# Gating normalizations put in order, two output tiles computed by token halves, and rotary tables started after the second latent weight

## The chip, the cores and the metric

The kernel runs on one core of a Trainium2 chip. The metric is the device time of one execution in microseconds (us). The engines of a core work side by side, each through its own queue in order: TensorE (PE, matmuls and transposes), VectorE (DVE), ScalarE (ACT), GpSimd (POOL) and SyncE (SP, which here only starts transfers). One engine waits for another by semaphores.

## The reference

Two layers run over a residual stream x of 1024 tokens by 1024 features, in float32.

```
for i in range(2):
    hn  = rms_norm(h, norm_mix[i])
    h  += mla(hn) if i == 0 else gmlp(hn)
    hn  = rms_norm(h, norm_ffn[i])
    h  += square(relu(hn @ ffn_w_up[i])) @ ffn_w_down[i]
    hn  = rms_norm(h, norm_ple[i])
    h  += sigmoid(hn @ ple_w_gate[i]) * (p[i] @ ple_w_proj[i])
```

Two parts matter here. The first is the start of `mla` (latent attention): `lat = hn @ w_down` gives 704 columns, 384 for the queries, 256 for keys and values, 64 for a rotary key; each part is normalized by its root mean square and the 64 are rotated by cos and sin of the token's position. The second is `gmlp`:

```
u, v = split(gelu(hn @ w_in))            # 2048 columns each
v  = layer_norm(v, ln_g, ln_b)           # over the 2048 columns of a token
sv = tril(w_s[g]) applied over the 128 tokens of a chunk, 8 groups g of 256 columns, + b_s
out = (u * sv) @ w_out
```

## The kernel before, in words

Every matrix is split into a high part of reduced float32 (fp32r) and a low part, the rest. A product is then three matmuls: high by high, high by low, low by high. `split(hi, lo, src)` does the splitting: ACT casts `src` to `hi` (line 111), DVE subtracts to get `lo` (line 112). A name that ends in h or l is such a part.

The program is written in one order and a scheduler of the language orders each engine's instructions from it, by priorities and estimated times; `tc.issue_after(ins)` is the one means by which the program itself pins what is issued under it behind a given instruction.

**Latent stage (first 50 us).** Eight blocks of 128 tokens: `block_x(b)` transposes a block on PE (tile `xp`, line 1088; two tiles of four transposes) and splits it (`xh`, `xl`); `square_x(b)` squares it on ACT (`xs`, line 1108) for the norm, and lets POOL add the parts (line 1109). `block_lat(b)` multiplies a block with the eight slices k of w_down (`lat`, line 65). Slice k of the weight is made when block 0 first needs it: ACT scales it to `wdh` (line 1065), DVE makes `wdl` (line 1066); of the last slice the two are one tile, `wdk`. Then ACT squares `lat` into `lats` with sums per token (line 1136), DVE turns the sums into reciprocal roots (`rl0v`, line 1496, with ACT's logarithm and exponential at 1497 and 1498) and scales `lats` (1141 to 1143), and `block_c(b)` transposes it on PE (`cp`, `cq`). The rotary tables come from `rope_tables`: DVE computes angles (`rw`, lines 1468 to 1472), ACT takes Abs and two Sin (1475 to 1477), DVE multiplies (`tab`, 1486 to 1489). A table load of ACT's function tables stands ahead of the Sins and another behind them (line 1288).

**Gating stage (about 1455 to 1915 us).** The second half of gelu(hn @ w_in), v, is computed first and parked in DRAM (`vpark`), with sums for the layer norm (`mv`, `rs`). Then four groups `gp` of 512 columns each run. Per group and block b of 128 tokens: `unit(b)` multiplies for u (`up`, ACT's gelu at line 894); `prep(b)` brings v back (`vr`, two blocks a transfer), normalizes it on DVE (line 884), multiplies by ln_g and adds ln_b on POOL (885, 886) and splits it into `vhl`; `spatial(b)` multiplies by w_s (`sv`) and DVE forms u·sv (line 908); `turn_y(b)` transposes that (`yp`, line 914) and splits it into `yh`, `yl`. At the end of a group `down_slice` multiplies yh, yl with four slices of w_out in eight output tiles `go` of 128 features by 1024 tokens, and DVE adds each into the residual (line 665). `go10` is group 1, tile 0. A matmul writes 512 tokens, so a tile has two halves c; a half needs the blocks 0 to 3 or 4 to 7 of y. `seq` makes the first tile of a group compute half 0 through all four k, and then half 1; every other tile does both halves at each k.

Of the kernel before, what the change touches and what calls it, by code (L numbers as in the profile page):

```python
# [16 lines left out]
P = 128  # L17
# [23 lines left out]
def trunk(ctx: ExitStack, tc: tile.TileContext, I, out):  # L41
# [68 lines left out]
    def split(hi, lo, src):  # L110
        S.copy(hi, src)  # L111
        V.tensor_tensor(lo, src, f32(hi), op=ALU.subtract)  # L112

# [24 lines left out]
    def gemm(blocks, rhs, f, name, seq=False, only=None):  # L138


        if only is not None:
            acc = {only: pso(name)}
            units = [(acc[only], CS[only])]
            csets = [(only,)]
        else:
            par[0] ^= 1
            if par[0]:
                full = psg(name)
                acc = [full[:, CS[c]] for c in range(2)]
                units = [(full, slice(0, T))] if not seq else [(acc[c], CS[c]) for c in range(2)]  # L150
            else:
                acc = [pso(f"{name}_{c}") for c in range(2)]
                units = [(acc[c], CS[c]) for c in range(2)]
            csets = [(0,), (1,)] if seq else [(0, 1)]
        nk = len(rhs)
        w = [(hi[:, kk, f * P:(f + 1) * P], lo[:, kk, f * P:(f + 1) * P]) for hi, lo in blocks for kk in range(hi.shape[1])]
        for cset in csets:
            for k, (wh, wl) in enumerate(w):
                for c in cset:
                    mm(acc[c], wh, rhs[k][c][0], k == 0, False)  # L160
                for c in cset:
                    mm(acc[c], wh, rhs[k][c][1], False, False)
                for c in cset:
                    mm(acc[c], wl, rhs[k][c][0], False, k == nk - 1)
        return units

    def chunked(hi, lo, n):
# [488 lines left out]
    def down_slice(w, k0, rhs, h, name, nxt, seq=False, before=None, after=None):  # L656
        bl = None
        for q in range(4):
            bl, ahead = bl or [load_block(w, k0, q * 256)], None
            for f in range(2):  # L660
                j = 2 * q + f
                if before is not None:
                    before(j)
                for u, c in gemm(bl, rhs, f, f"{name}{j}", seq and j == 0):
                    V.tensor_tensor(h[j][:, c], u, h[j][:, c], op=ALU.add)  # L665
# [116 lines left out]
    def gmlp(h, nrm, nxt, after):  # L782
# [83 lines left out]
        rs = rsqrt_small(mv[:, :, 1], EPS, "lnr")  # L866

        for gp in range(4):
            f0 = gp * 512
# [6 lines left out]
            vhl = tmp(f"vhl{gp}", [P, 2, 512], F32R)  # L876
            us, vr = {}, {}

            def prep(b):
# [3 lines left out]
                v = vr[0][:, b % 2]  # L883
                V.tensor_scalar(v, v, mv[:, b, 0:1], rs[:, b:b + 1], op0=ALU.subtract, op1=ALU.mult)
                G.tensor_tensor(v, v, gb[:, 0], op=ALU.mult)
                G.tensor_tensor(v, v, gb[:, 1], op=ALU.add)
                split(vhl[:, 0], vhl[:, 1], v)

# [21 lines left out]
            def turn_y(b):  # L910
# [4 lines left out]
                bs = slice(b * P, (b + 1) * P)  # L915
                split(yh[:, :, bs], yl[:, :, bs], pp.rearrange("p (j t) -> p j t", t=P))

# [84 lines left out]
    def mla(h, park):  # L1002
        w_down, w_uq, w_ukv, w_out = (I[n][0] for n in ("mla_w_down", "mla_w_uq", "mla_w_ukv", "mla_w_out"))
        with tc.tile_pool(name="pm", bufs=1) as pm:
# [108 lines left out]
            def block_lat(b):  # L1113
# [3 lines left out]
                for k in range(KT):  # L1117
# [10 lines left out]
                    if k == 6 and b in late_x:  # L1128
                        square_x(b, *late_x[b])
                    if k == KT - 1 and b == 0:  # L1130
                        rotary()
                    yield
# [153 lines left out]
            def rotary():  # L1286
                with tc.issue_after(rope_tables(tab, pos, gq, inv).ins):
                    table.append(S.preload_act_table_set(LNEXP))
                gains_turn(*gb, 16)
                V.scalar_tensor_tensor(gqk, gT[:, 48:49], SCALE, gT[:, 49:50], op0=ALU.mult, op1=ALU.mult)  # L1290
# [283 lines left out]
```

## Time and profile before

| what | us |
|---|---|
| three runs | 2656.77, 2651.12, 2653.01 (median 2653.01) |
| the profiled execution | 2655.07 |
| its span, from first to last instruction | 2653.3 |
| PE busy | 2595.6 |
| DVE busy | 1480.3 |
| ACT busy | 1040.1 |
| POOL busy | 322.8 |
| mean granted clock of PE, of 1 | 0.995 |

The span is that of the profiler's record of one execution. PE is busy for nearly all of it, so the questions to the trace are where PE has no work, what ended each such wait, and where its granted clock is under 1. Durations below are read from this one execution. Successive instructions of one engine overlap in the record, so that the starts of neighbours can be closer than the duration of one.

### The profile page before, as it was taken

The numbers are of one execution on the slowest core, as the hardware profiler recorded it, in microseconds if no ns is written. First come the engines' busy times: TensorE is split into PE (matmuls) and PEld (weight loads), VectorE is DVE, ScalarE is ACT, GpSimd is POOL, SyncE is SP. The second block draws the span as 40 slices with busy tenths as digits, with TensorE's granted clock in tenths as the row PEclk, the third lists the DMA queues.
The fourth block names the chain that finished last, engine by engine and source line by source line (L and its number), as shares of the span: only waits on it lengthen the run. The fifth ranks groups of instructions, "written<-read, shape, count | busy, mean of one in ns | idle before, by whom it ended". The sixth has DMA issues, their size and how long they took to land. (4 is left out here: it accounts for less than half of the span.)

```text
span 2653.3 us, 33181 instructions
## 1 busy us (share of the span) xinstructions
PE 2595.6 (98%) x12736; PEld 2193.9 (83%) x12736; DVE 1480.3 (56%) x2396; ACT 1040.1 (39%) x2109; POOL 322.8 (12%) x460
## 2 busy tenths in 40 slices
PE   7999999999999999999999999999999999999999
PEld 7988888878888888888888787888788888888887
DVE  5677775886565434375522545336966654444641
ACT  4576773654443212164522312214644441221430
POOL 4544431000000000001211433030000000000000
PEclk9999999999999999999999999999999999999999
DMA  5200002233345323233232312212333362332220
GB/s 163 71 8 21 25 25 88 96 119 104 127 151 190 115 68 111 64 100 90 86 111 95 101 39 88 77 43 96 98 125 111 120 228 97 112 111 64 80 76 36
DMA packets 211341, 247.41 MB, mean 93 GB/s; under 512 B 9792, under 2 KB 159872, under 8 KB 211184
## 3 DMA queue, kind: packets, MB, share of 16 engines
q1 hardware_dynamic: 206368, 230.21, 26.9%
q0 software_dynamic: 4816, 15.10, 1.9%
q8 instruction: 100, 1.64, 0.3%
q14 instruction: 57, 0.47, 0.1%
HBM read 186.55 MB, written 58.72 MB: 92 GB/s over the span
## 5 line engine op out<-in xcount | busy, mean ns | idle before, releaser
L111 ACT CAST wh<-raw 128x1024 fp32r<-128x1024 f32 x96 | 100.9, 1051 | 390.8 <-PE f0d L65 130.3
L665 DVE TENSOR_TENSOR f0h<-f0d,f0h 128x512 f32<-128x512 f32 (+1 forms) x84 | 70.4, 866 | 166.0 <-PE f0d L65 166.0
L665 DVE TENSOR_TENSOR f1h<-f1d,f1h 128x512 f32<-128x512 f32 (+1 forms) x84 | 70.4, 865 | 157.5 <-PE f1d L65 157.5
L112 DVE TENSOR_TENSOR wl<-raw,wh 128x1024 fp32r<-128x1024 f32 x96 | 117.8, 1227 | 56.5 <-ACT wh L111 50.3
L744 POOL TENSOR_TENSOR f0h<-sig,f0h 128x512 f32<-128x512 f32 x16 | 21.9, 1388 | 846.1 <-DVE sig L743 827.4
L65 PE MATMUL go<-yl,wh 128*128 128x512 f32 x256 | 84.3, 395 | 2.7 <-DVE yl L112 2.7
L824 DVE BATCH_NORM_STATS2 vst<-vg 128x6 f32<-128x512 f32 (+1 forms) x40 | 23.3, 586 | 113.5 <-ACT vg L823 113.4
L65 PE MATMUL go<-yh,wh 128*128 128x512 f32 x256 | 84.6, 395 | 0.0
L65 PE MATMUL go<-yh,wl 128*128 128x512 f32 x256 | 83.3, 392 | 0.0
L894 ACT ACTIVATE u<-up,n_r 128x512 f32<-128x512 f32 x32 | 22.0, 687 | 155.4 <-PE up L65 155.2
L665 DVE TENSOR_TENSOR f0h<-go,f0h 128x512 f32<-128x512 f32 (+1 forms) x52 | 40.4, 809 | 63.6 <-PE go L65 63.6
L65 PE MATMUL s<-kT,q 128*128 128x512 f32 (+5 forms) x288 | 72.8, 355 | 2.4 <-DVE q L112 1.8
L823 ACT ACTIVATE vg<-vp,n_r 128x512 f32<-128x512 f32 (+1 forms) x40 | 24.0, 603 | 122.9 <-PE vp L65 121.5
L65 PE MATMUL av<-pt,v 128*128 128x256 f32 (+1 forms) x480 | 64.1, 284 | 5.2 <-DVE sm L1375 2.7
L65 PEld LDWEIGHTS av<-pt,v 128*128 128x128 f32 x480 | 59.9, 191 | 8.1 <-issue 3.7
L1376 POOL TENSOR_SCALAR p<-p,sm 128x128 f32<-128x128 f32 (+3 forms) x64 | 49.2, 770 | 86.8 <-DVE sm L1375 55.3
L65 PEld LDWEIGHTS go<-yl,wh 128*128 128x128 f32 x256 | 48.4, 189 | 13.3 <-DVE yl L112 3.8
L65 PE MATMUL f1d<-f_ah,wh 128*128 128x512 f32 x192 | 59.3, 390 | 0.0
L65 PE MATMUL f0d<-f_ah,wh 128*128 128x512 f32 x192 | 59.2, 390 | 0.0
L65 PE MATMUL f0d<-f_al,wh 128*128 128x512 f32 x192 | 59.2, 389 | 0.0
L65 PE MATMUL f1d<-f_al,wh 128*128 128x512 f32 x192 | 59.2, 389 | 0.0
L65 PE MATMUL f1d<-f_ah,wl 128*128 128x512 f32 x192 | 59.1, 389 | 0.0
(5412 smaller groups left out, 8029.2 us busy)
## 6 DMA issues: line engine op xcount, KB each, us to landing
raw<-in_ffn_w_down_dram SPq DMA_DIRECT2D x56, 512.0 KB, 3.6
f0ar<-f_apark SPq DMA_DIRECT2D x32, 512.0 KB, 3.5
f1ar<-f_apark SPq DMA_DIRECT2D x32, 512.0 KB, 3.4
raw<-in_ffn_w_down_dram SPq DMA_DIRECT2D x32, 256.0 KB, 3.0
raw<-in_ple_w_gate_dram SPq DMA_DIRECT2D x16, 512.0 KB, 4.1
vr<-vpark SPq DMA_DIRECT2D x16, 512.0 KB, 4.4
raw<-in_gmlp_w_out_dram SPq DMA_DIRECT2D x16, 512.0 KB, 3.5
vpark<-vg POOLq DMA_DIRECT2D x24, 256.0 KB, 2.3
```

The lines of the kernel that those rows point to most:

```text
L65: PE.matmul(o, l, r, start=start, stop=stop)
L111: S.copy(hi, src)
L112: V.tensor_tensor(lo, src, f32(hi), op=ALU.subtract)
L665: V.tensor_tensor(h[j][:, c], u, h[j][:, c], op=ALU.add)
L744: G.tensor_tensor(h[j][:, cs], sg, h[j][:, cs], op=ALU.add)
L823: last = S.activation(t, o, AF.Gelu_apprx_tanh, scale=nrm.r[:, b:b + 1])
L824: V.bn_stats(vst[:, b, cc], t)
L894: S.activation(us[b][:, b % 2], o, AF.Gelu_apprx_tanh, scale=r[:, b:b + 1])
L1376: G.tensor_scalar(pr_[:, :n], pr_[:, :n], sm[:, 2:3], 1.0, op0=ALU.mult, op1=ALU.mult)
```

## The change

There are three parts. In `gmlp` each normalization on DVE is pinned by `behind`: block 0's behind the last subtraction for yl of the group before (none in the first group), block 1's behind block 0's subtraction for vhl, every further block's behind that of two blocks before. For that `split` returns its DVE instruction. In `down_slice`, for the first pair of tiles of each group, the new `gemm_pair` computes the first half of tile 0, the first half of tile 1, the second half of tile 0 and the second half of tile 1. In `block_lat`, `rotary()`, now without the transposition of the later gains, is called behind slice 1 of block 0 and not behind slice 7; the gains keep their place in `later_gains()`.

```diff
     def split(hi, lo, src):
         S.copy(hi, src)
-        V.tensor_tensor(lo, src, f32(hi), op=ALU.subtract)
+        return V.tensor_tensor(lo, src, f32(hi), op=ALU.subtract).ins
+
+    @contextmanager
+    def behind(ins):
+
+        if ins is None:
+            yield
+        else:
+            with tc.issue_after(ins):
+                yield
...
+    def gemm_pair(blocks, rhs, name):
+
+        full = psg(f"{name}0")
+        acc = [[full[:, CS[c]] for c in range(2)], [pso(f"{name}1_{c}") for c in range(2)]]
+        w = [(hi[:, kk], lo[:, kk]) for hi, lo in blocks for kk in range(hi.shape[1])]
+        for c in range(2):
+            for f in range(2):
+                fs = slice(f * P, (f + 1) * P)
+                for k, (wh, wl) in enumerate(w):
+                    mm(acc[f][c], wh[:, fs], rhs[k][c][0], k == 0, False)
+                    mm(acc[f][c], wh[:, fs], rhs[k][c][1], False, False)
+                    mm(acc[f][c], wl[:, fs], rhs[k][c][0], False, k == len(w) - 1)
+        return {f: [(acc[f][c], CS[c]) for c in range(2)] for f in range(2)}
...
             bl, ahead = bl or [load_block(w, k0, q * 256)], None
+            units = {}
+            if seq and q == 0:
+                units = gemm_pair(bl, rhs, name)
             for f in range(2):
...
-                for u, c in gemm(bl, rhs, f, f"{name}{j}", seq and j == 0):
+                for u, c in units.get(f) or gemm(bl, rhs, f, f"{name}{j}"):
...
+        y_last = [None]
         for gp in range(4):
...
-            us, vr = {}, {}
+            us, vr, done = {}, {}, {}
...
                 v = vr[0][:, b % 2]
-                V.tensor_scalar(v, v, mv[:, b, 0:1], rs[:, b:b + 1], op0=ALU.subtract, op1=ALU.mult)
+                with behind(y_last[0] if b == 0 else done.get(0 if b == 1 else b - 2)):
+                    V.tensor_scalar(v, v, mv[:, b, 0:1], rs[:, b:b + 1], op0=ALU.subtract, op1=ALU.mult)
                 G.tensor_tensor(v, v, gb[:, 0], op=ALU.mult)
                 G.tensor_tensor(v, v, gb[:, 1], op=ALU.add)
-                split(vhl[:, 0], vhl[:, 1], v)
+                done[b] = split(vhl[:, 0], vhl[:, 1], v)
...
-                split(yh[:, :, bs], yl[:, :, bs], pp.rearrange("p (j t) -> p j t", t=P))
+                y_last[0] = split(yh[:, :, bs], yl[:, :, bs], pp.rearrange("p (j t) -> p j t", t=P))
...
+                    if k == 1 and b == 0:
+                        rotary()
                     if k == KT - 1 and b == 0:
-                        rotary()
+                        later_gains()
...
             def rotary():
                 with tc.issue_after(rope_tables(tab, pos, gq, inv).ins):
                     table.append(S.preload_act_table_set(LNEXP))
+
+            def later_gains():
                 gains_turn(*gb, 16)
```

DVE at the start of the gating stage, before (vr00 holds blocks 0 and 1 of group 0, vr02 blocks 2 and 3; x2 are two such instructions in a row):

```order
L884 TENSOR_SCALAR vr00_13041<-vr00_13041,mv_12964,lnrr_12974 128x512 x2
L884 TENSOR_SCALAR vr02_13131<-vr02_13131,mv_12964,lnrr_12974 128x512 x2
L884 TENSOR_SCALAR vr04_13228<-vr04_13228,mv_12964,lnrr_12974 128x512 x2
L884 TENSOR_SCALAR vr06_13325<-vr06_13325,mv_12964,lnrr_12974 128x512 x2
L112 TENSOR_TENSOR vhl0_12987<-vr00_13041,vhl0_12987 128x512
L908 SCALAR_TENSOR_TENSOR u00_13013<-sv00_13048,bst_12464,u00_13013 128x256 x2
L112 TENSOR_TENSOR vhl0_12987<-vr00_13041,vhl0_12987 128x512
L112 TENSOR_TENSOR wl93_13379<-raw93_13376,wh93_13378 128x1024
```

The same place of the changed kernel:

```order
L912 TENSOR_SCALAR vr00_13041<-vr00_13041,mv_12964,lnrr_12974 128x512
L112 TENSOR_TENSOR vhl0_12987<-vr00_13041,vhl0_12987 128x512
L912 TENSOR_SCALAR vr00_13041<-vr00_13041,mv_12964,lnrr_12974 128x512
L912 TENSOR_SCALAR vr02_13131<-vr02_13131,mv_12964,lnrr_12974 128x512
L936 SCALAR_TENSOR_TENSOR u00_13013<-sv00_13048,bst_12464,u00_13013 128x256 x2
L112 TENSOR_TENSOR vhl0_12987<-vr00_13041,vhl0_12987 128x512
L912 TENSOR_SCALAR vr02_13131<-vr02_13131,mv_12964,lnrr_12974 128x512
L112 TENSOR_TENSOR wl93_13379<-raw93_13376,wh93_13378 128x1024
```

One normalization now stands ahead of block 0's low half, and the others stand one behind each later low half.

PE at the end of group 1, before, behind the last transposes for block 7 of y and three products of go11_0 (go10 and go11 are output tiles 0 and 1, go11_0 and go11_1 the halves of tile 1):

```order
L65 MATMUL go11_0_14066<-yl1_13643,wh97_14035 128x512
L65 MATMUL go10_14039<-yh1_13642,wh97_14035 128x512
L65 MATMUL go11_1_14067<-yh1_13642,wh97_14035 128x512
L65 MATMUL go11_0_14066<-yh1_13642,wl97_14036 128x512
L65 MATMUL go11_0_14066<-yh1_13642,wh97_14035 128x512
L65 MATMUL go10_14039<-yl1_13643,wh97_14035 128x512
L65 MATMUL go10_14039<-yh1_13642,wl97_14036 128x512
```

The same place of the changed kernel, behind the last transposes and nine products of go11_0:

```order
L65 MATMUL go11_0_14040<-yl1_13643,wh97_14035 128x512
L65 MATMUL go11_0_14040<-yh1_13642,wl97_14036 128x512
L65 MATMUL go10_14039<-yh1_13642,wh97_14035 128x512
L65 MATMUL go10_14039<-yl1_13643,wh97_14035 128x512
L65 MATMUL go10_14039<-yh1_13642,wl97_14036 128x512
```

Between the transposes and the first product of go10 with yl1, the first that reads block 7 of yl1, stand twelve products now, eleven of go11_0, where eight stood.

DVE at the same place, before (u16 is u of blocks 6 and 7, vr20 the first transfer of group 2):

```order
L112 TENSOR_TENSOR yl1_13643<-yp16_14010,yh1_13642 128x4x128
L908 SCALAR_TENSOR_TENSOR u16_13933<-sv17_14017,bst_12464,u16_13933 128x256 x2
L884 TENSOR_SCALAR vr20_14355<-vr20_14355,mv_12964,lnrr_12974 128x512
L112 TENSOR_TENSOR yl1_13643<-yp17_14026,yh1_13642 128x4x128
L884 TENSOR_SCALAR vr20_14355<-vr20_14355,mv_12964,lnrr_12974 128x512
```

And of the changed kernel (f0h1 is residual tile 1):

```order
L112 TENSOR_TENSOR yl1_13643<-yp16_14010,yh1_13642 128x4x128
L936 SCALAR_TENSOR_TENSOR u16_13933<-sv17_14017,bst_12464,u16_13933 128x256 x2
L112 TENSOR_TENSOR yl1_13643<-yp17_14026,yh1_13642 128x4x128
L912 TENSOR_SCALAR vr20_14355<-vr20_14355,mv_12964,lnrr_12974 128x512
L691 TENSOR_TENSOR f0h1_8483<-go11_0_14040,f0h1_8483 128x512
```

The low half of block 7 is no longer behind a normalization of group 2, and only one normalization is left there.

DVE in the latent stage, before, from slice 2 of the weight on:

```order
L1066 SCALAR_TENSOR_TENSOR wdl2_245<-wdraw0_161,gT_94,wdh2_244 128x704
L1066 SCALAR_TENSOR_TENSOR wdl5_288<-wdraw1_162,gT_94,wdh5_287 128x704
L1066 SCALAR_TENSOR_TENSOR wdl3_255<-wdraw0_161,gT_94,wdh3_254 128x704
L1066 SCALAR_TENSOR_TENSOR wdl6_304<-wdraw1_162,gT_94,wdh6_303 128x704
L1066 SCALAR_TENSOR_TENSOR wdk7_324<-wdraw1_162,gT_94,wdk7_324 128x704
L1468 TENSOR_TENSOR rw_333<-pos_221,inv_121 128x256
L1482 TENSOR_SCALAR gq_118<-gq_118 128x64
L99 COPY gT_94<-gps16_358 128x34
L1469 TENSOR_SCALAR rw_333<-rw_333 128x256
L1290 SCALAR_TENSOR_TENSOR gqk_95<-gT_94 128x1
L1138 TENSOR_SCALAR v00_373<-ss00_313 128x1
```

And of the changed kernel, from slice 1 on:

```order
L1094 SCALAR_TENSOR_TENSOR wdl1_235<-wdraw0_161,gT_94,wdh1_234 128x704
L1500 TENSOR_TENSOR rw_244<-pos_221,inv_121 128x256
L1514 TENSOR_SCALAR gq_118<-gq_118 128x64
L1094 SCALAR_TENSOR_TENSOR wdl4_297<-wdraw1_162,gT_94,wdh4_296 128x704
L1501 TENSOR_SCALAR rw_244<-rw_244 128x256
L1094 SCALAR_TENSOR_TENSOR wdl2_270<-wdraw0_161,gT_94,wdh2_269 128x704
L1502 TENSOR_SCALAR rw_244<-rw_244 128x256
L1094 SCALAR_TENSOR_TENSOR wdl5_313<-wdraw1_162,gT_94,wdh5_312 128x704
L1504 SCALAR_TENSOR_TENSOR rw_244<-rw_244 128x256
L1094 SCALAR_TENSOR_TENSOR wdl3_280<-wdraw0_161,gT_94,wdh3_279 128x704
L1504 SCALAR_TENSOR_TENSOR rw_244<-rw_244 128x256
L1094 SCALAR_TENSOR_TENSOR wdl6_329<-wdraw1_162,gT_94,wdh6_328 128x704
```

The angles' operations have moved between the weight's subtractions. ACT runs Abs, the table loads and the Sins in the same order as before, directly behind the last slice of the weight, but block 0's xs stands one slice earlier and the first cast of block 2 stands ahead of the squares of `lat0`.

## Rows read from the trace of the kernel before

**Rows 1.** The page, busy time of TensorE: us, share of the span, instructions.

```profile
PE 2595.6 (98%) x12736; PEld 2193.9 (83%) x12736; DVE 1480.3 (56%) x2396; ACT 1040.1 (39%) x2109; POOL 322.8 (12%) x460
```

**Rows 2.** Waits of PE: engine, line, waited for; total us, times, longest us.

```profile
PE yp L914 <- DVE u L908: 4.6, 3, 1.8
PE sv L65 <- DVE vhl L112: 4.4, 1, 4.4
PE cp L1151 <- ACT lats L1136: 4.2, 1, 4.2
...
PE go L65 <- DVE yl L112: 2.7, 2, 1.4
...
PE lat L65 <- ACT wdh L1065: 2.5, 1, 2.5
```

**Rows 3.** Timeline of PE, latent stage: start us, us, instruction, idle before.

```profile
28.90 0.49 PE L65 MATMUL lat<-wdk,xl 128*128 128x384 f32 x2
...
33.08 1.04 PE L1088 MATMUL xp<-idf,x 128*128 128x128 f32 x8
38.27 1.09 PE L1151 MATMUL cp<-idf,lats 128*128 128x128 f32 x4 [4.15 <-ACT lats L1136]
```

**Rows 4.** Timeline of ACT, latent stage.

```profile
28.23 0.42 ACT L1475 ACTIVATE rw<-rw 128x256 f32<-128x256 f32 x1 [5.71 <-DVE rw L1472]
...
32.09 0.49 ACT L1136 ACTIVATE lats<-lat 128x384 f32<-128x384 f32 x1
```

**Rows 5.** Timeline of DVE, latent stage.

```profile
22.64 3.09 DVE L1066 SCALAR_TENSOR_TENSOR wdk<-wdraw,gT,wdk 128x704 fp32r<-128x704 f32 x1
...
26.84 1.35 DVE L1472 SCALAR_TENSOR_TENSOR rw<-rw 128x256 f32<-128x256 f32 x3
...
34.45 1.89 DVE L1496 TENSOR_SCALAR rl0v<-ssl,v 128x3 f32<-128x3 f32 x1 [0.26 <-ACT lats L1136]
```

**Rows 6.** Timeline of POOL, latent stage.

```profile
21.82 3.16 POOL L1109 TENSOR_TENSOR xs<-xh,xl 128x1024 f32<-128x1024 f32 x1 [14.07 <-ACT xs L1108]
...
33.79 2.52 POOL L1109 TENSOR_TENSOR xs<-xh,xl 128x1024 f32<-128x1024 f32 x1 [7.57 <-ACT xs L1108]
```

**Rows 7.** Windows: stretch, us; busy us (count) of five engines; granted clock; DMA.

```profile
19.20:24.00 4.80, 4.80 (x20) 4.80 (x21) 4.80 (x5) 3.31 (x5) 2.18 (x1) 0.64 0.33 105
38.27:43.80 5.53, 5.53 (x21) 5.53 (x22) 5.09 (x13) 2.42 (x9) 3.29 (x3) 0.50 0.54 158
1476.57:1481.20 4.63, 4.63 (x16) 3.76 (x17) 1.98 (x3) 0.62 (x1) 4.63 (x4) 0.63 0.09 22
1524.69:1529.20 4.51, 4.51 (x15) 3.73 (x16) 2.92 (x5) 0.59 (x1) 1.73 (x2) 0.62 0.42 154
```

**Rows 8.** Timeline of DVE, first gating group.

```profile
1465.31 9.53 DVE L884 TENSOR_SCALAR vr<-vr,mv,lnrr 128x512 f32<-128x512 f32 x8
1474.77 1.74 DVE L112 TENSOR_TENSOR vhl<-vr,vhl 128x512 fp32r<-128x512 f32 x1
```

**Rows 9.** Timeline of POOL, first gating group.

```profile
1465.94 2.95 POOL L885 TENSOR_TENSOR vr<-vr,gb 128x512 f32<-128x512 f32 x2 [2.94 <-DVE vr L884]
1468.86 2.90 POOL L886 TENSOR_TENSOR vr<-vr,gb 128x512 f32<-128x512 f32 x2
```

**Rows 10.** Timeline of ACT, first gating group.

```profile
1470.36 0.62 ACT L111 CAST vhl<-vr 128x512 fp32r<-128x512 f32 x1 [3.04 <-POOL vr L886]
```

**Rows 11.** Timeline of PE, first gating group.

```profile
1476.57 0.39 PE L65 MATMUL sv<-vhl,wsh 128*128 128x256 f32 x1 [4.42 <-DVE vhl L112]
```

**Rows 12.** Timeline of DVE, an iteration without weight splits.

```profile
1505.57 0.69 DVE L112 TENSOR_TENSOR yl<-yp,yh 128x512 fp32r<-128x512 f32 x1 [4.48 <-ACT yh L111]
...
1506.97 0.68 DVE L112 TENSOR_TENSOR vhl<-vr,vhl 128x512 fp32r<-128x512 f32 x1
1512.20 0.69 DVE L112 TENSOR_TENSOR yl<-yp,yh 128x512 fp32r<-128x512 f32 x1 [4.55 <-ACT yh L111]
```

**Rows 13.** Timeline of DVE, tail of the second group.

```profile
1627.27 0.55 DVE L884 TENSOR_SCALAR vr<-vr,mv,lnrr 128x512 f32<-128x512 f32 x1 [2.62 <-DMA vr<-vpark]
```

More of the change, by code (lines that the diff above doesn't have):

```diff
@@ L1 @@
-from contextlib import ExitStack
+from contextlib import ExitStack, contextmanager
 import concourse.bass as bass
```

## The prediction

> **What bounds the kernel now.** The page's busy line comes first: TensorE (PE) is busy 2595.6 us [rows 1] of a span of 2653.3, so only 57.7 us of the span are not matmul, and only a gap of PE, or matmuls that run slowly, can be won. The table of PE's waits comes second: the four groups that lie where the diff works are 4.6 (yp), 4.4 (sv), 4.2 (cp) and 2.7 us (go) [rows 2]. The reader is to see that sv and cp are one wait each, yp three and go two. Third come the timelines around each of them, to see what ended the wait, and fourth the granted clock just behind it. That view shows a second cost: behind some gaps PE works at the lower of its two levels (1.2 instead of 2.4 GHz, 0.50 in the rows). A stretch of busy time b at mean grant g holds work for b·g at full speed, so it lost b·(1−g): behind cp 5.53·0.50 = 2.77 us, behind sv 4.63·0.37 = 1.71, behind the first yp wait 4.51·0.38 = 1.71, and behind an early wait of 2.5 on a weight [rows 2] 4.80·0.36 = 1.73 [rows 7].
>
> **Part 1, first gating group: the normalizations in order.** Before, DVE runs all eight normalizations of group 0 in one block, 1465.31 to 1474.84, 9.53 us or 1.19 each, where one alone takes 0.55 [rows 8, 13]: POOL's multiplications and additions run all the while, 2.95 us a pair from 1465.94 and from 1468.86 [rows 9]. The high half of block 0 is cast by ACT at 1470.36 [rows 10], but the low half (vhl on DVE) stands behind the eight, 1474.77 to 1476.51 [rows 8], and PE starts at 1476.57 after 4.42 us [rows 11]: it had been ready at 1472.15. In the changed order one normalization stands ahead of that low half. It ends at 1465.86; POOL multiplies to about 1467.4 (1.47 each, half of a pair) and adds from there, or from 1468.86 at the latest, when the addition ran before, to 1470.3 at the latest; ACT's cast (0.62) and DVE's subtraction (0.68 as in [rows 12]) follow: 1471.6, half a microsecond ahead of 1472.15. So the whole wait goes: **−4.4**. Were the low half held by POOL as before (1.74 instead of 0.68), 0.5 would stay. What is late next is block 1: normalized behind the low half of block 0, with block 2's multiplication ahead of its addition on POOL: three POOL operations (4.4), cast and subtraction (1.3 to 2.4) from about 1472.2 give 1478 to 1479. PE reaches it one iteration after 1472.15, 6.6 us by the distance between two yl, 1505.57 and 1512.20 [rows 12], or 1478.7. I take no wait and keep 0.5 for the range. Without the gap, the slow stretch behind it has no gap to follow: **−1.7**, ends 0 and −1.71 [rows 7].
>
> In all later iterations a normalization, its two POOL operations, a cast and a subtraction have two iterations to finish in, since block b waits for block b−2's low half: 0.55 + 2.95 + 0.62 + 0.68 = 4.8 us of 13.2. DVE is idle some 4.5 of each iteration [rows 12], so the 0.55 that each gets is hidden. The cover would be gone if a block took a whole iteration longer.
>
> **Part 2, the tails of groups 0 to 2.** PE's order up to the last transposes (yp of block 7) is as before, and so are its 4.6 us for u: they stay, **0**, and with them, as I take it, the slow stretch in group 0 (end −1.71). Behind them, in groups 1 and 2, PE waits once more, 2.7 us in the two, 1.4 the longer [rows 2]. The reason is on DVE: the low half of y (yl) stood behind a normalization of the next group that itself waited 2.62 for its DMA and ran 1627.27 to 1627.82 [rows 13]. The change acts twice: the next group's first normalization now goes behind yl, and between the last transposes and the first product that reads the new yl PE has twelve products to do, eleven of them of output tile 1, where it had eight (both counted in the order). At 0.24 each (an iteration of PE is 24 products of 512 columns, six of 256 and four of 128, as much as 28 of 512, in 6.63 us by [rows 12]) four more are 0.95 us. And yl comes at least 0.5 earlier, by the normalization's own time, and more, since DVE stood idle for 2.62 in front of it. 0.95 + 0.5 is as much as the wait, so the two go: **−2.7**, end −1.4 if one of the two groups still waits. Tile 0's second half comes one half-tile's products later (12 at 0.24, 2.9 us), tile 1's first half earlier by as much; DVE has that time, except in group 3, where the residual's adds are followed by the next norm. There I bound it by ±1 and take **0**. The normalizations that leave the tail for the next group's iterations free DVE there; nobody waits for it.
>
> **Part 3, the rotary tables earlier.** PE finishes the latent product of block 0 at 29.39 [rows 3], but ACT squares it only at 32.09, since Abs, two table loads and two Sin stand ahead: from Abs at 28.23 to that square it is 3.86 us [rows 4]. Abs waited for DVE's three rw operations at 26.84 [rows 5], which stood behind a weight split (wdk) that ran 3.09 us beside POOL's xs, 21.82 to 24.98 [rows 5, 6]. In the changed order the rw operations stand between the splits. POOL's xs comes one ACT cast earlier (about 0.8, so to 24.2) and now holds a split with one rw left behind it; after it come two splits and two rw (0.75, the wdk row beyond 24.98, and 0.45, a third of [rows 5]): Abs at about 26.8, and ACT free of the tables at 30.7, 1.4 earlier. Seven of the eight transposes of block 2 move ahead of the end of the latent products, 0.13 each [rows 3], so block 0's product ends near 30.3: covered. A cast of block 2's transposes now stands ahead of the squares (0.6, as the cast of the same shape in [rows 10]), which leaves 0.8. Next in line is rl0v on DVE: it ran 34.45 to 36.34 because POOL's second xs held it, 33.79 to 36.31 [rows 5, 6], and cp began 1.93 behind its end. That xs comes as much earlier as the squares, so it still ends the wait: **−0.8**. Ends: 0, if the splits that are pushed back stop PE for as long; −2.4, if rl0v is no longer held as well: it had been ready to run at 34.45, so without the hold some 1.6 more would go. The gap of 4.15 [rows 3] becomes about 3.3; the nearest row is the gap of 2.5, behind which 1.73 was lost instead of 2.77 [rows 2, 7]: **−1.0**, ends 0 and −2.77.
>
> DVE's lock against POOL is the place for a rule that speaks against the change. The eight normalizations beside POOL took 1.19 each, the single one 0.55 [rows 8, 13]; the low half took 1.74 beside POOL and 0.68 in a later iteration [rows 8, 12]. The Trainium skill, "SBUF — State Buffer", section "SBUF: two separate sides", says that a vector operation with two SBUF inputs, and a GpSimd one, exclude one another for a whole instruction. These rows agree; by that rule the change moves 24 blocks' POOL work from the tails, beside adds that read one operand from PSUM, into the iterations, beside subtractions that read both from SBUF. What it would make of the time is the third rival.
>
> **The sum.** −4.4 −1.7 −2.7 −0.8 −1.0 = −10.6. The profiled execution took 2655.07 us, 1.8 beyond its span, and becomes 2644.5. It stood 2.06 above the median of the runs, 2653.01; on that footing the forecast is **2642.4 us**.
>
> **Rivals.**
> *Only the idle time goes.* The slow stretches recur elsewhere and the latent stage gives nothing back: 2653.01 − 7.1 = 2645.9; with half of go as well lost 2647.3. For it: a slow stretch also followed the longest yp wait, of only 1.8 [rows 2, 7], and such waits remain. Against: behind sv and cp the gap itself goes or shrinks.
> *The slow stretches go altogether,* that of the first tail too, and rl0v is no longer held: −2.4 −2.8 −4.4 −1.7 −1.7 −2.7 = −15.7, 2637.3. For it: the stretch in the tail has the shortest of the four gaps; against: the latent gap, by the sum, stays over the 2.5 that sufficed.
> *POOL beside the splits (slower).* The subtraction of each block is held by POOL and PE waits for it in 31 of 32 iterations. A hold by one POOL operation is up to 1.47 and DVE's idle 4.5 stands against it, so this decides only if POOL's in-order pairs put the chain of a block over its iteration. From 10.6/31 = 0.34 us a block the change is no gain; over 0.51 it is measurably slower; at 1.0 us it is 2642.4 + 31 = 2673.4.
> *The waits turn into others.* POOL's or the DMA's lateness ends the go waits and sv's as before (the vr transfer lands when it did), and only the latent stage moves: 2653.01 − 1.8 = 2651.2. Against: the order shows yl ahead of what waited.
>
> **How the numbers follow.** About 0.2% (5.3 us) is what a measurement of this kernel can tell from no change. Chances: forecast 0.60 (2639 to 2645), idle only 0.17, all slow stretches 0.12, POOL beside the splits 0.05, turned waits 0.06. Faster: the first three but for a sixth of "idle only" and a bit of the forecast, 0.85; within 0.2% 0.11; slower 0.04. The range 2635.5 to 2648.5 takes in the ends −15.7 with one more for group 3, and −4.5 (little more than the gap of sv), and leaves out the last two rivals.
>
> **What would show it.** In the waits of PE after: sv gone, go gone, yp still near 4.6, cp near 3; full clock behind sv; a low half of about 0.7 to 1.2 in the iterations, with no sv wait among them. Abs near 27 and squares near 31. It is wrong if sv appears many times (POOL), if cp still waits 4 us or more, or if the clock drops in places where it did not.

## The result, and the profile after

The changed kernel took 2640.13 us (median of five runs, 2637.74 to 2643.83) against 2653.01 for the kernel before, a ratio of 0.9949 with a 95% interval of 0.9938 to 0.9961. That is 12.9 us less, where 10.6 were forecast. The profiled execution took 2643.83 us, with a span of 2641.8.

PE's waits after, as engine, line, waited for, total us, times, longest:

```profile
PE xp L1116 <- DMA x<-in_x_dram: 6.7, 2, 4.6
...
PE yp L942 <- DVE u L936: 4.4, 3, 1.6
...
PE cp L1181 <- ACT lats L1166: 2.5, 1, 2.5
...
PE f1u0g L416 <- ACT n4T L111: 1.6, 1, 1.6
...
PE lat L65 <- DVE wdl L1094: 1.2, 1, 1.2
```

Of the four groups of [rows 2] sv and go are gone, yp stands almost as it was, and cp has fallen from 4.2 to 2.5. A wait for a weight split (lat for wdl) is new, and the wait for the transfer of x at the start is longer by 2.8 in this execution.

The totals hide where the time went, so PE's timelines were laid side by side at points that both have (start times, us):

| first matmul of | before | after | difference |
|---|---|---|---|
| the latent products | 10.17 | 13.08 | +2.91 |
| cp, block 0 | 38.27 | 36.76 | −1.51 |
| the rotary key's transposes | 95.81 | 93.40 | −2.41 |
| mla's output product | 412.85 | 412.66 | −0.19 |
| sv, group 0 | 1471.87 | 1472.26 | +0.39 |
| the last product of u with wu0h (group 0) | 1517.17 | 1511.29 | −5.88 |
| up, group 1 | 1567.38 | 1559.69 | −7.69 |
| up, group 2 | 1667.15 | 1657.79 | −9.36 |
| up, group 3 | 1766.85 | 1755.89 | −10.96 |
| the second feed-forward's last down phase | 2177.75 | 2166.18 | −11.57 |

So in this execution the gating stage gave everything: 6.27 us inside group 0, and 1.81, 1.67 and 1.60 at the three tails. The latent stage began 2.9 late, was 1.5 ahead at cp and 2.4 ahead at its end, and attention lost 2.2 of that again. The late start is not the change's: the latent products begin at 8.8 to 10.7 us in six profiles and at 12.7 to 13.4 in the seven others, with the rotary part (e3 10.2, the changed kernel 13.1) and without it (the kernel before 10.2, e1 13.2). By cp it had cost little, because in the kernel before PE then waited 2.5 for a weight, with a slow stretch behind it [rows 2, 7], and in the changed kernel 0.6 with a granted clock of 1.00 behind.

**Group 0.** DVE at the start, which answers [rows 8] (start us, us, instruction, idle before):

```profile
1465.70 0.55 DVE L912 TENSOR_SCALAR vr<-vr,mv,lnrr 128x512 f32<-128x512 f32 x1
1469.68 0.69 DVE L112 TENSOR_TENSOR vhl<-vr,vhl 128x512 fp32r<-128x512 f32 x1 [3.43 <-ACT vhl L111]
1470.29 1.00 DVE L912 TENSOR_SCALAR vr<-vr,mv,lnrr 128x512 f32<-128x512 f32 x2
...
1475.62 1.11 DVE L112 TENSOR_TENSOR vhl<-vr,vhl 128x512 fp32r<-128x512 f32 x1 [1.57 <-ACT vhl L111]
```

One normalization of 0.55 stands ahead of the low half of block 0, which runs 1469.68 to 1470.37 and not 1474.77 to 1476.51. Block 1's low half ends at 1476.73, two microseconds before PE asks for it. The granted clock behind sv answers the third of [rows 7] (stretch, us, busy us of PE, PEld, DVE, ACT and POOL, granted clock, DMA):

```profile
1472.26:1482.00 9.74, 9.74 (x52) 8.31 (x51) 3.27 (x5) 3.21 (x5) 6.50 (x6) 1.00 0.16 54
1518.59:1523.00 4.41, 4.41 (x22) 3.73 (x23) 2.17 (x4) 0.58 (x1) 1.50 (x2) 1.00 0.52 192
```

PE is busy for the whole of the first stretch at clock 1.00. The second stretch is the tail of group 0, where [rows 7] showed 0.62; there too the slow stretch is gone, though a yp wait of 1.6 still stands ahead of it.

**Tail of group 1** on DVE, which answers [rows 13]:

```profile
1614.42 1.23 DVE L112 TENSOR_TENSOR wu2l<-wu2r,wu2h 128x1024 fp32r<-128x1024 f32 x1 [0.33 <-ACT wu2h L111]
1615.57 0.68 DVE L112 TENSOR_TENSOR yl<-yp,yh 128x512 fp32r<-128x512 f32 x1
1616.17 0.87 DVE L936 SCALAR_TENSOR_TENSOR u<-sv,bst,u 128x256 f32<-128x256 f32 x2
1618.25 0.69 DVE L112 TENSOR_TENSOR yl<-yp,yh 128x512 fp32r<-128x512 f32 x1 [1.22 <-ACT yh L111]
1619.68 0.55 DVE L912 TENSOR_SCALAR vr<-vr,mv,lnrr 128x512 f32<-128x512 f32 x1 [0.74 <-DMA vr<-vpark]
```

The low half of block 7 (yl, 1618.25) now begins 1.4 us ahead of the normalization, which still has to wait for its transfer. What stands ahead of u (1616.17), a weight split of 1.22 and yl of block 6, is as before, and so is yp's wait.

**Latent stage.** DVE and POOL, which answer [rows 5, 6]:

```profile
21.39 2.62 DVE L1504 SCALAR_TENSOR_TENSOR rw<-rw 128x256 f32<-128x256 f32 x1
23.94 0.94 DVE L1094 SCALAR_TENSOR_TENSOR wdl<-wdraw,gT,wdh 128x704 fp32r<-128x704 f32 x1
...
26.33 0.94 DVE L1094 SCALAR_TENSOR_TENSOR wdk<-wdraw,gT,wdk 128x704 fp32r<-128x704 f32 x1
...
33.16 1.75 DVE L1528 TENSOR_SCALAR rl0v<-ssl,v 128x3 f32<-128x3 f32 x1
```

```profile
21.33 2.41 POOL L1137 TENSOR_TENSOR xs<-xh,xl 128x1024 f32<-128x1024 f32 x1 [13.58 <-ACT xs L1136]
...
32.50 2.38 POOL L1137 TENSOR_TENSOR xs<-xh,xl 128x1024 f32<-128x1024 f32 x1 [7.53 <-ACT xs L1136]
```

POOL's first xs held the first rw of line 1504 for 2.62 instead of a weight split; the next split (23.94) was late by that, and PE waited 1.15 for it. POOL's second xs held rl0v for 1.75. On ACT, which answers [rows 4]:

```profile
26.45 0.42 ACT L1507 ACTIVATE rw<-rw 128x256 f32<-128x256 f32 x1 [3.65 <-DVE rw L1504]
...
30.79 0.50 ACT L1166 ACTIVATE lats<-lat 128x384 f32<-128x384 f32 x1
```

Abs came 1.8 us earlier and the square of block 0's latent product 1.3.

### The profile page after: what moved, and what is told of

Its sections match the earlier page's. It is cut to its first block, busy times and chain, and to the rows that moved or that the text cites. A ratio compares the mean times of both kernels' runs of the same rounds, so it can differ in the third digit from the quotient of the medians.

```text
span 2641.8 us, 33164 instructions
## 1 busy us (share of the span) xinstructions
PE 2592.4 (98%) x12736; PEld 2192.0 (83%) x12736; DVE 1469.6 (56%) x2396; ACT 1039.2 (39%) x2109; POOL 314.5 (12%) x460
## 4 chain that ended last, share of the span: by engine, by line
PE 64%; DVE 4%; ACT 2%; DMA 1%; issue 0%; ACTq 0%; DVEq 0%
PE f0d L65 13%; PE f1d L65 12%; PE vp L65 7%; PE up L65 6%; PE go L65 5%; PE e L65 4%; PE pg L65 3%; PE pj L65 1%; PE sv L65 1%; PE f1u6g L416 1%; PE f1u7g L416 1%; PE f1u15g L416 1%; PE f1u14g L416 1%; PE f1u13g L416 1%; PE f1u12g L416 1%; PE f1u11g L416 1%
## 5 line engine op out<-in xcount | busy, mean ns | idle before, releaser
L913 POOL TENSOR_TENSOR vr<-vr,gb 128x512 f32<-128x512 f32 x32 | 42.0, 1317 | 246.4 <-DVE vr L912 246.4
L65 PE MATMUL f0d<-f_ah,wl 128*128 128x512 f32 x192 | 59.1, 389 | 0.0
```

The lines of the kernel that those rows point to most:

```text
L65: PE.matmul(o, l, r, start=start, stop=stop)
```

## The experiments

Each kernel is compared with runs of the kernel before on the same chip; medians in us. The changed kernel was not run again beside them: where its median of 2640.13 is named below, the kernel before stood at 2653.01.

| kernel | median | before | ratio, 95% interval |
|---|---|---|---|
| e1, the order alone | 2641.69 | 2652.92 | 0.9960, 0.9947 to 0.9972 |
| e2, the pair alone | 2650.14 | 2652.92 | 0.9989, 0.9980 to 0.9998 |
| e3, the rotary tables alone | 2650.03 | 2652.92 | 0.9992, 0.9983 to 1.0001 |
| e4, order and pair | 2643.18 | 2652.92 | 0.9961, 0.9949 to 0.9974 |
| e5, the gap at cp filled | 2638.53 | 2652.96 | 0.9944, 0.9930 to 0.9958 |
| e6, POOL's additions pinned | 2639.96 | 2652.96 | 0.9950, 0.9935 to 0.9966 |
| e7, weight block behind y | 2636.75 | 2652.96 | 0.9938, 0.9925 to 0.9951 |
| e8, POOL's work doubled | 2675.62 | 2652.96 | 1.0082, 1.0067 to 1.0096 |
| e9, POOL's additions wait | 2636.48 | 2654.05 | 0.9934, 0.9919 to 0.9949 |
| e10, e7 and e9 | 2634.22 | 2654.05 | 0.9928, 0.9915 to 0.9940 |
| e11, one more POOL operation | 2640.74 | 2654.05 | 0.9952, 0.9939 to 0.9966 |

**The parts one by one (e1 to e4).** In e1 the new tile pair is not used and `rotary()` is back at the last slice; e2 has `behind(None)` and `rotary()` back; e3 has `behind(None)` and no pair; e4 has `rotary()` back only.

```diff
-                    if k == 1 and b == 0:
-                        rotary()
                     if k == KT - 1 and b == 0:
+                        rotary()
                         later_gains()
...
-                with behind(y_last[0] if b == 0 else done.get(0 if b == 1 else b - 2)):
+                with behind(None):
...
-            if seq and q == 0:
-                units = gemm_pair(bl, rhs, name)
...
```

> Only the gating normalizations are put in order; first tile pair and rotary tables as before. Theory (the order alone clears the gating stage): no sv wait (4.4 before), no slow stretch behind it (1.7), and go waits of at most 0.2 us each instead of 1.4 and 1.3, since the low half of y no longer stands behind a normalization that waits for its transfer; cp still waits 4.2. In all -8.5 to -10, about 2643.5 to 2644.5. Rival (the paired tiles carry the tails): go still waits 1 us or more in both groups, total -6.1, about 2647.

> Only the first two output tiles of each group are computed by token halves. Theory (the order alone clears the gating stage): sv waits 4.4 as before, go about 0.4 to 0.7 in each of the two groups because yl still stands behind a normalization that waits for its transfer; total -1 to -2, about 2651 to 2652. Rival (the paired tiles carry the tails): no go wait, -2.7, about 2650.3.

> Only the rotary tables are started behind slice 1. Theory (the latent stage gives what its gap and clock show): cp waits about 2.5 instead of 4.2, slow stretch behind it half as long, the transposes of block 0 and all behind them -2.4 by 50 us, and -2.4 at the end, about 2650.6. Rival (what is won there is given back by slow stretches in attention, three of which stand in the changed kernel at 224, 304 and 384 us and one in the kernel before): -0.2 at 430 us, and 2652 to 2653 in all.

> The two gating parts without the rotary part. Theory (latent stage is worth what its gap and clock show): about 2.4 us behind the full change, 2642.5; attention with one slow stretch, at about 228. Rival (given back in attention): equal to the full change within 0.5 us, 2640.1, because attention loses 2 us only with the rotary part.

Laid against the kernel before as in the table above, from the first sv to the last down phase of the second feed-forward, the gating stage gave 12.43 us with the order alone, 4.77 with the pair alone, 1.53 with neither (e3), 12.18 with both in e4 and 11.96 in the changed kernel. Up to the start of group 3 the five are 11.10, 3.80, 1.23, 11.37 and 11.35; the rest lies behind, nearly all in the second feed-forward. e3's gating stage is the one of before, so 1.2 to 1.5 is what two executions differ by. The order alone does all that the two do. The pair by itself shortens the tails by 1.26, 1.33 and 1.23, where e3 has 0.59, −0.03 and 0.68, and nothing is left for it once yl comes early. PE's waits in the stage in e1, and in e2:

```profile
PE yp L939 <- DVE u L933: 4.4, 3, 1.6
```

```profile
PE sv L65 <- DVE vhl L112: 4.4, 1, 4.4
PE yp L942 <- DVE u L936: 4.2, 3, 1.5
PE go L65 <- DVE yl L112: 0.4, 1, 0.4
```

e1 has no go wait at all. e2 has one left, of 0.4, in group 0. The theory that the order alone clears the stage holds for e1. For e2 it was too pessimistic, since go was expected to wait 0.4 to 0.7 in both groups; the rival, that the pair carries the tails, is refuted by e1. e1 came out 2 us faster than expected.

e3 shows why the tails gave 5.1 and not 2.7. Its tails have the order of before, and in group 0:

```profile
1522.68 0.44 PE L939 MATMUL yp<-idf,u 128*128 128x128 f32 x2 [1.44 <-DVE u L933]
...
1526.51 0.50 PE L65 MATMUL go<-yl,wh 128*128 128x512 f32 x1 [1.06 <-DVE yl L112]
```

In this execution no slow stretch follows yp, and a go wait of 1.06 stands there instead. In the profile of before PE worked at 0.62 there, took 1.71 longer for the products ahead of go, and so found yl ready. The slow stretch had hidden a third go wait. What the changed kernel's profile gained in group 0 is thus mainly that stretch of the before's execution, which neither e2 nor e3 has; laid against e3, the three tails gave 1.22, 1.70 and 0.92, or 3.84 in all.

e3 and e4 also answer the question of attention. e3 was 1.57 ahead at the last cp and 1.58 at the end of attention, so nothing was given back, and e4 has no slow stretch in attention; the rival, that the rotary part costs slow stretches there, does not hold, since e3 has one like the kernel before. By 50 us e3 was expected to be 2.4 ahead; it was 0.90 ahead at block 0's cp and 1.57 at the rotary key. Its median is 2.9 under the before's (2650.6 was expected), although the interval reaches 1.0001. e4 was expected to lose 2.4 and lost 3.1 against the changed kernel's median; the two intervals overlap, so that size is not settled by them.

**Is the clock the gap's doing? (e5)** Nine products that nobody reads stand in the gap ahead of cp.

```diff
...
+                    fl = pso("fill")
+                    with tc.issue_after(lat_end[1]):
+                        for j in range(9):
+                            mm(fl, idr, wd[0][0][:, :512], j == 0, j == 8)
```

> The changed kernel with nine extra products (a unit matrix from w_down's first slice, into a tile that nobody reads) on PE between the last latent product of block 1 and cp. Theory (slow stretches are made by the gap in front of them): the gap at cp shrinks from 2.5 to under 0.6, no slow stretch stands behind it, cp begins within 0.5 of where it did, and from 50 us on PE is about 1.7 earlier than in the changed kernel. Rival (the slow stretch comes at a time of its own, or from the load of all engines): full or longer slow stretch at 37 to 41 us, no gain.

The stretch behind cp in the changed kernel, and in e5 with the filled gap ahead of it:

```profile
36.76:41.00 4.24, 4.24 (x19) 4.22 (x20) 4.19 (x8) 2.11 (x8) 2.76 (x2) 0.60 0.78 211
```

```profile
34.50:37.16 2.66, 2.25 (x12) 1.56 (x10) 2.05 (x6) 1.80 (x8) 1.67 (x2) 1.00 0.36 145
37.16:41.40 4.24, 4.24 (x27) 4.17 (x28) 4.19 (x8) 2.12 (x8) 2.76 (x2) 1.00 0.75 211
```

0.60 became 1.00 with 19 and 27 matmuls in the same 4.24 us; the gap that was left is 0.41. From cp to the rotary key's transposes PE needed 55.48 us and not 56.64, 1.2 less, where 1.7 had been expected. But one execution of e5 does not show that the filling did it. e8 and e11 below leave the latent stage as it is in the changed kernel; their cp, and the stretch behind it, e8 first:

```profile
35.83 0.63 PE L1183 MATMUL cp<-idf,lats 128*128 128x128 f32 x4 [2.44 <-ACT lats L1168]
...
36.65 0.63 PE L1182 MATMUL cp<-idf,lats 128*128 128x128 f32 x4 [2.45 <-ACT lats L1167]
```

```profile
35.83:40.07 4.24, 4.24 (x28) 4.22 (x29) 4.19 (x8) 2.12 (x8) 2.76 (x2) 1.00 0.78 211
36.65:40.89 4.24, 4.24 (x28) 4.22 (x29) 4.19 (x8) 2.12 (x8) 2.75 (x2) 1.00 0.79 211
```

The gap is the changed kernel's 2.46, nothing fills it, and the clock stays at 1.00; from cp to the rotary key these two need 55.42 and 55.13 us. Over all thirteen profiles a slow stretch stands at cp with each of the four gaps of 4.2 to 5.7 us, with four of the six of 2.3 to 2.5 (the changed kernel, e3, e6, e7) and with none of the three of 0.4 to 1.6 (e5, e9, e10). That shorter gaps have fewer slow stretches fits the theory; the one run of e5 fits the rival as well, and the question stays open. In total e5 stands 1.6 under the changed kernel's median, within the scatter of the runs.

**Does POOL hold DVE? (e6, e9)** e6 pins POOL's two additions with `tc.issue_after` behind DVE's instructions.

```diff
...
+                    if k == 7 and b in stores:
+                        with tc.issue_after(wd_ins[7] if b == 0 else scaled[0]):
+                            stores[b]()
```

> The changed kernel with POOL's two additions of the latent stage (xs of blocks 0 and 1) moved behind the last weight split and behind the scaling of block 0. Theory (POOL's long addition holds DVE's rl0v and the rotary's second rw): that rw takes 0.4 instead of 2.6, rl0v 0.2 instead of 1.75, PE's wait for a weight split (1.15) goes, and cp begins 1.5 to 2.7 us earlier, with a gap of 0.3 to 1.5 instead of 2.5. Rival (rl0v is late for its sums on ACT, its long record is a wait): rl0v still ends at about 34.9 and cp at 36.8.

It failed as an experiment: each engine's order came out as in the changed kernel, POOL began its additions as soon as its operands were there (20.50 and 31.66), rw took 2.60 and rl0v 1.75. Here the pin set the order within an engine and made no other engine wait. What e6 is good for is a further profile of the same instructions (median 2639.96), with one slow stretch in attention (222 to 230) where the changed kernel's profile had three, and 2.80 us ahead of before at attention's end where that was 0.2. The three stretches thus belong to that execution.

In e9 POOL first copies one column of what DVE is to have finished.

```diff
...
+                        late = const.tile([P, 1], F32, name=f"late{b}")
+                        src = f32(wd[7][1])[:, :1] if b == 0 else kr[:, 0, :1]
+                        with tc.issue_after(G.tensor_copy(late, src).ins):
+                            stores[b]()
```

> The changed kernel with POOL's two additions of the latent stage really made to wait: a one-column copy on POOL reads the last weight split (for block 0) and the rotary key of block 0 (for block 1) ahead of them. Theory (POOL's long addition holds DVE's rl0v and the rotary's second rw): rw 0.4 instead of 2.6, rl0v 0.2 instead of 1.75, no wait of PE for a weight split, cp 2 to 3 us earlier against the start of the latent products, its gap 0.3 to 1.0, and no slow stretch at 36 to 41: about -2 to -4 in all, 2636.5 to 2638. Rival (rl0v's long record is a wait for its sums): rl0v ends as before and cp's gap stays 2 us or more.

```profile
21.43 0.42 DVE L1517 SCALAR_TENSOR_TENSOR rw<-rw 128x256 f32<-128x256 f32 x1
...
26.79 1.56 DVE L1523 TENSOR_TENSOR rw<-rw 128x256 f32<-128x256 f32 x1 [1.35 <-ACT rw L1521]
...
32.39 0.22 DVE L1541 TENSOR_SCALAR rl0v<-ssl,v 128x3 f32<-128x3 f32 x1
```

```profile
25.65 2.41 POOL L1141 TENSOR_TENSOR xs<-xh,xl 128x1024 f32<-128x1024 f32 x1
...
35.12 2.40 POOL L1141 TENSOR_TENSOR xs<-xh,xl 128x1024 f32<-128x1024 f32 x1
```

```profile
34.48 0.63 PE L1194 MATMUL cp<-idf,lats 128*128 128x128 f32 x4 [1.56 <-ACT lats L1179]
```

```profile
34.48:39.00 4.52, 4.52 (x30) 4.50 (x31) 4.47 (x7) 2.11 (x8) 3.70 (x4) 1.00 0.32 91
```

rl0v took 0.22 (0.21 in e10) and rw 0.42, the wait for a weight split is gone, cp began 2.3 us earlier than in the changed kernel, and no slow stretch follows (with a gap of 1.56; see e5). What POOL's addition now meets is the first rw behind the Sins (26.79), which took 1.56, to 28.35, while POOL was busy to 28.06: the hold moved with the addition. The Trainium skill, "SBUF — State Buffer", section "SBUF: two separate sides", says that a DVE operation with two SBUF inputs and a GpSimd operation that reads SBUF exclude one another, and that the one that starts first has the shared port for its whole instruction. The rw, with two inputs in SBUF, agrees. rl0v, and the normalizations of [rows 8], read one tensor and a scalar per partition and were held too; for such operations the section names a 2-port mode of DVE, and no trace here shows whether they ran in it. cp's gap was 1.56, more than the 0.3 to 1.0 expected: rl0v comes behind the tables, at which DVE works without a pause from 28.26 on, the end of that hold. The median is 3.7 under the changed kernel's, though the two intervals overlap.

**What is left in the tails (e7).** ACT's cast of the next group's second weight block goes behind yh of block 6, DVE's subtraction behind yl of block 7.

```diff
...
-            split(hi, lo, raw)
+            if hold is not None and k0 == 6:
+                casts["hold"] = casts["y6"]
+                with behind(hold):
+                    split(hi, lo, raw)
...
-                w = [t for part in load_cols(w_in, f0, f"wu{gp}", "x") for t in part]
+                w = [t for part in load_cols(w_in, f0, f"wu{gp}", "x", y_last[0]) for t in part]
```

> The changed kernel with the second weight block of the next group (its cast behind yh of block 6, its subtraction behind yl of block 7) moved out of the way of u of block 7. Theory (the yp waits that are left come from that weight split ahead of u on DVE): the three yp waits fall from 1.6, 1.4 and 1.4 to about 0.5 each, about -3 in all, 2637. Rival (u is late for the product sv or for its own operands): waits stay at 1.4 each.

```profile
PE yp L951 <- DVE u L945: 1.5, 3, 0.5
```

yp's three waits fell from 4.4 to 1.5, as the theory had it, and the three tails are 2.9 shorter than in the changed kernel's profile. The median is 3.4 under the changed kernel's, with intervals that overlap. What the remaining 0.5 at each tail waits for, no run takes apart.

**How far POOL's work is covered (e8, e11).** e8 subtracts ln_b from each block and adds it again; e11 multiplies each block by one.

```diff
                 G.tensor_tensor(v, v, gb[:, 1], op=ALU.add)
+                G.tensor_tensor(v, v, gb[:, 1], op=ALU.subtract)
+                G.tensor_tensor(v, v, gb[:, 1], op=ALU.add)
```

> The changed kernel with POOL's work for each block of v doubled: ln_b is subtracted and added once more. Theory (a block has two iterations to be ready, so POOL's work is covered): no sv wait from block 2 on, 0 to 2 us in all from block 1 of group 0, and not over 3 us slower than the changed kernel. Rival (POOL beside the splits): sv waits in most of the 32 iterations, 10 us or more slower.

```profile
PE yp L944 <- DVE u L938: 16.4, 6, 4.9
PE sv L65 <- DVE vhl L112: 5.0, 8, 0.7
PE sv L65 <- ACT vhl L111: 3.8, 4, 3.4
```

```profile
1565.00:1618.00 53.00, 50.96 (x247) 41.98 (x247) 24.72 (x36) 15.25 (x23) 40.00 (x30) 1.00 0.16 50
```

Theory and rival both missed the size: the median is 35.5 us over the changed kernel's, and the two profiles differ by 27.2. Waits for sv are only 8.8 of it, and 3.35 of these are one wait for block 1 of group 0. The larger part is in the tails: 13.6 of yp's 16.4 us stand there, with a slow clock at each of the three. The next group's weight block came late: its cast on ACT began at 1518.07, after waiting 3.43 for the transfer, 2.8 later than in the changed kernel (1515.23), while PE's last product with wu0h came only 0.5 later. The transfers of POOL and of that weight block in the changed kernel, and in e8:

```profile
1505.85 0.57 POOL L898 DMA_DIRECT2D gb<-in_gmlp_ln_g_dram  x1 [0.89 <-POOL vr L914]
...
1511.34 0.37 SPq L804 DMA_DIRECT2D wu1r<-in_gmlp_w_in_dram  x1
```

```profile
1511.44 0.57 POOL L898 DMA_DIRECT2D gb<-in_gmlp_ln_g_dram  x1 [0.89 <-POOL vr L916]
...
1511.85 0.37 SPq L804 DMA_DIRECT2D wu1r<-in_gmlp_w_in_dram  x1
```

The weight block's transfer started 0.5 later than there, as PE's product did, so its buffer was free in time; but it landed 6.2 us after its start and not 3.9, and at the two other tails 7.0 and 7.2 after it and not 3.7 and 3.6. In e8 POOL comes to the next group's ln_g and ln_b, which it transfers itself, only behind its doubled work, and so issues them 0.4 us ahead of the weight block; in the changed kernel it issues them 5.5 us ahead of it. That these transfers slow one another is the likely cause; no run moves them alone. POOL was busy for 40.0 of 53 us in the stretch of the second group above, and in the first group for 35.28 of 40 (19.29 in the changed kernel).

```diff
                 G.tensor_tensor(v, v, gb[:, 1], op=ALU.add)
+                G.tensor_scalar(v, v, 1.0, 1.0, op0=ALU.mult, op1=ALU.mult)
```

> The changed kernel with one more POOL operation for each block of v (a multiplication by one). Theory (POOL's occupancy sets the cover: two operations leave room, four cost 35 us): with three, about 4.2 us of an iteration's 6.6, no sv waits from block 2 on, 0 to 4 us slower than the changed kernel. Rival (each additional POOL operation holds DVE in every iteration): half of what doubling cost, 15 to 18 us slower.

The added operation took only 0.62, not the 1.3 reckoned with, so POOL's work grew from 2.6 to 3.2 a block; no sv wait came, and the median is 0.6 over the changed kernel's. So a loss begins somewhere between 3.2 and 5.2 us of POOL's time a block, of an iteration of 6.6.

**Both improvements (e10).**

> The weight block behind y and POOL's latent additions made to wait, together. Theory (they are separate places): -3.4 as measured for the first and -2 to -4 for the second, 2632.5 to 2635. Rival (the latent stage's gain is lost again in attention, as in the profile of the changed kernel): no better than the first alone, 2636.7.

2634.22, below each alone (the intervals overlap) and 5.9 under the changed kernel's median; it is the fastest version that was run, with yp waits of at most 0.5 and no slow stretch at cp or in attention. It was expected at 2632.5 to 2635.

## Why the prediction was right, and where its terms were off

The forecast was 2642.4 and 2640.13 was measured: the signs of all terms held. The sizes of the tails and of the cp gap did not, and parts of the agreement are luck.

- **sv and the clock behind it** (−4.4 and −1.7): 6.27 measured against 6.1. Block 0's low half ended at 1470.37, 1.9 us ahead of PE; the prediction's latest case was 1471.6. The addition began at 1467.71 and not at 1468.86, the latest that was allowed for. That the later iterations have no sv wait held too.
- **The tails** (−2.7, with group 0 at 0): 5.08. This is the step that failed, in two sizes. In group 0 the slow stretch behind the yp wait was let stay (0, end −1.71), and no go wait was counted, since the profile showed none. The stretch did not come back, and group 0 gave 1.81; e3 showed that the stretch belonged to the one execution of before and had hidden a go wait of 1.06. So some of the 5.08 is luck: against e3 it is 3.84. In groups 1 and 2 the two parts of the change were taken as each doing a share of the wait, 0.95 and at least 0.5; e1 showed that the order alone clears it. The low half of block 7 starts 1.55 us behind the end of the yp wait in group 1 and not 3.42, and 1.4 ahead of the normalization, for which the idle 2.62 us in [rows 13] had been the sign. The pair costs nothing and adds nothing measurable.
- **yp** (0): 4.4 after 4.6, as predicted; e7 shows that its cause is the weight block ahead of u.
- **The latent stage** (−0.8 and −1.0): cp 1.51 earlier although the latent products began 2.91 later, and −2.41 by the rotary key, where −1.8 was forecast; of two profiles that began alike, before and e3, it is −0.90 and −1.57. The gap became 2.46, not 3.3. The slow stretch behind it lost 1.70 (4.24·0.40) instead of 2.77, a gain of 1.07 as forecast from the nearest row. That this size fits is luck in part: two of the six profiles with such a gap have no slow stretch there. The path was not quite the one drawn: POOL's first xs held an rw and not a split; the end "splits that are pushed back stop PE" came to pass with 1.15 us on PE, and ACT was free at 30.3, earlier than the 30.7 reckoned. That rl0v is held by POOL's second xs, as the step said, e9 shows: 1.75 with POOL beside it, 0.22 without.
- **Group 3** (0 ± 1): from the last up of group 3 on nothing beyond 0.6 moved, in the up phase of the second feed-forward.
- **The slower rival** (0.05): at this kernel's 2.6 us of POOL's time a block it did not come. With doubled work some iterations wait for sv (e8), so the text's bound, that a block would have to take an iteration longer, was too generous: POOL was 88% busy in the first group. But most of e8's loss came at the tails, by late transfers, a path that the prediction does not have.

What stays open: the median gained 12.9 us and the profiled executions 11.24 (2655.07 to 2643.83), and the slow stretches of attention, none, one or three of them in profiles of kernels whose attention is the same, are one reason why single executions differ by 2 us; why they come and go no run explains. The same holds for the stretch at cp, and with it for what filling a gap is worth.

## What to carry to other kernels

Read a scheduler's order for what a late instruction stands behind, and not only for what it depends on: one operation of 0.5 us that waits for a transfer can cost the engine that waits for the instruction behind it 1.1 to 1.4 us, at each of three places. A gap of the engine that bounds a kernel costs more than its length where a slow clock follows it, and a slow clock can itself hide the next wait; so after a change count the waits that a full clock would uncover. A slow stretch in one profile may belong to that execution alone: look for another execution with the same gap before crediting an edit with its absence. And where two edits address one wait, run each alone before keeping both.

## What the runs showed of the hardware

- A DVE operation on 128x3 values that takes 0.22 us took 1.75 (changed kernel) and 1.89 (before) beside one addition on POOL; when that addition was moved, the operation took 0.22 and another one beside it was held (e9).
- The granted clock behind a gap of 2.3 to 2.5 us ahead of cp was 0.60 to 0.66 over 4.24 us in four profiles (the changed kernel, e3, e6, e7) and 1.00 in two (e8, e11); behind 4.2 to 5.7 us it was 0.50 to 0.67 in all four, behind 0.4 to 1.6 us 1.00 in all three.
- On POOL a multiplication of 128x512 values by a constant took 0.62 us where an addition of two such operands took 1.29 (e11).
- A transfer of 512 KB that was issued 0.4 to 1.0 us behind the first of POOL's two transfers took 6.2 to 7.2 us to land; issued 5.5 to 6.1 us behind it, it took 3.6 to 3.9 (e8, and the changed kernel).
